# Linear attention on alternating row and column halves, an earlier first product in the convolution, a later first spreading

## The chip, the cores and the metric

The kernel runs on one core of one Trainium2 chip. The metric is the device time of one execution in microseconds; of several runs the median counts. Engines are named as in the profile: PE is TensorE's matmuls, PEld its weight loads, DVE VectorE, ACT ScalarE, POOL GpSimd, SP the engine that issues most loads.

## The reference

Two blocks act on a sequence of 512 frames of width 1024. Cut to the stages that the change touches:

```python
def gla_chunked(q, k, v, g_log):          # 4 heads, key width 64, value width 128, chunks of 64
    q_dec = qc * jnp.exp(bc); k_dec = kc * jnp.exp(-bc)
    A = jnp.einsum('bhnck,bhnsk->bhncs', q_dec, k_dec)
    A = jnp.where(tril, A, 0.0)
    o_intra = jnp.einsum('bhncs,bhnsv->bhncv', A, vc)
    dS = jnp.einsum('bhnck,bhncv->bhnkv', kc * jnp.exp(b_last - bc), vc)
    ...                                    # scan: S = decay * S + dS
    o_inter = jnp.einsum('bhnck,bhnkv->bhncv', q_dec, s_prev)
    o = o_intra + o_inter

def parallel_mixer(xn, ...):
    proj = xn @ w_in                       # xn = rms_norm(h)
    ...                                    # fox attention; gla_chunked; rms_norm of both per head
    return jnp.concatenate([fox_out, gla_o * silu(gr)], axis=-1) @ w_out

def conformer_conv(x, ...):
    a = glu(x @ w_pw1 + b_pw1); y = depthwise_conv(a, width 31) + b_dw
    return silu(layernorm(y, ln_g, ln_b)) @ w_pw2 + b_pw2
```

Around them stand memory cross attention, an MLP, two gated feed-forward blocks and banded attention, which the change leaves alone.

## The kernel before

Activations lie feature-major: eight tiles of 128 features by 512 frames. A dense product is done three times in fp32r, on a high and a low part of both operands (mm3: L396, L397, L398 in the profile), as 128x512 matmuls. Weights come as tiles of 512 KB (raw), one load each on SP's queue; ACT casts the high part (wH, L374) and DVE subtracts the low part (wL, L375), up to four units ahead.

PE runs in the order in which the program is written. In the mixer a helper, drive, mixes a stage (a generator) with a queue of dense products: each yield of the stage gives a number, and dense products are put in until they make up for it. ACT, DVE and POOL get their order from a scheduler, which goes by the program's dependences; in the convolution's second half it is as written.

gla_front does the first norm and the projections of linear attention (GLA). The input norm's factor is a row of 512 numbers; it is spread to all partitions by two matmuls against diagonal tiles: diagonal_pair makes eight 128x128 tiles dg (L1305, DVE), spread multiplies them with ones (L1312) and copies the result to rbc. z, the narrow product times rbc (L945), feeds L960; the narrow product (L465) packs four groups of 32 columns into the array.

gla_back takes GLA's chunks. state(c) adds up one chunk of 64 frames: four matmuls with 64 rows (frames) and 64 columns (keys of a head), to one bank. scores(bp, j) takes two blocks of 128 frames and the two heads on row half j: four matmuls of 64 rows, 128 columns. Behind them, per (bp, j), four times: one full matmul of the masked scores att with gv (L1077), then two quarter matmuls, qd with the states sprev, one for each column half (L1081). ACT copies each output bank to oo (L1084), head_norm squares, sums and scales oo (L742, L743, L751; odd rows on POOL), and L1093 transposes oo to features. The queries and keys of fox attention go through head_norm as well (tm_rows at L732, then L757 transposes them). All of these small products are in plain FP32, in which the trace shows two passes a matmul.

In the convolution, pc sums the taps (L1418, 72 passes of 128x128 in its last group). Layer norm then gives cY (L1551), turn(t) transposes tile t (L1556), gate(t) applies the activation on ACT (cz, L1561) and splits the tile (L540, L541), and the second projection, fm_steps on four banks with their weights W, takes one tile k at a time. keep_warm (L473) runs products on a constant tile, as many as WARM says: at the program's start, ahead of the first transposes, and after those of tile 2.

Of the kernel before, what the change touches and what calls it, by code (L numbers as in the profile page):

```python
# [21 lines left out]
P = 128  # L22
# [45 lines left out]
WARM = (16, 14, 8)  # L68
# [203 lines left out]
class Builder:  # L272
# [653 lines left out]
    def gla_front(self, pool, chl, selr, E):  # L926
# [11 lines left out]
        more(2, G1, 8)  # L938
        rb = self.spread(dg)
# [15 lines left out]
        more(3)  # L955
# [66 lines left out]
    def gla_back(self, pool, gm, E):  # L1022
# [9 lines left out]
        def scores(bp, j):  # L1032
            rs = slice(j * 64, j * 64 + 64)
            att = pool.tile([P, 2, 2, P], F32, tag="att", name=self.nm("att"), bufs=4)
            nc.gpsimd.memset(att, 0.0)
            ps = self.bank().rearrange("p (a t c) -> p a t c", a=2, t=2)
            for a in range(2):
                ts = slice((2 * bp + a) * P, (2 * bp + a + 1) * P)
                for t in range(2):
                    nc.tensor.matmul(ps[:, a, t, :], lhsT=kd[rs, t, ts], rhs=qd[rs, t, ts], start=True, stop=True)  # L1040
            nc.vector.copy_predicated(att, gm.unsqueeze(1).unsqueeze(1).to_broadcast([P, 2, 2, P]), ps)
            atts[bp, j] = att


        def state(c):
            b, rs = c // 2, slice((c % 2) * 64, (c % 2) * 64 + 64)
            ps = self.bank()
            for t in range(2):
                for j in range(2):
                    hs, h = slice(j * 64, j * 64 + 64), 2 * t + j  # L1050
                    nc.tensor.matmul(ps[hs, t * P:(t + 1) * P], lhsT=k2t[rs, b, t, hs], rhs=gv[rs, b, h * P:(h + 1) * P],
                                     start=True, stop=True)
            for t in range(2):
                src = ps[:, t * P:(t + 1) * P]
                if c == 0:
                    nc.vector.tensor_copy(sprev[:, t, 1, :], src)
                else:
                    nc.vector.scalar_tensor_tensor(sprev[:, t, c + 1, :], sprev[:, t, c, :], dec[:, t, c:c + 1], src,
                                                   ALU.mult, ALU.add)

        for c in range(7):
            state(c)
            if c >= 3:
                scores((c - 3) // 2, (c - 3) % 2)
            yield 2.0
        on = []
        for bp in range(2):
            oo = [self.tmp([P, 2, 2, P], name="oo") for _ in range(2)]
            for j in range(2):
                rs = slice(j * 64, j * 64 + 64)  # L1070
# [303 lines left out]
    def ph_con(self, ph):  # L1374
        nc, tc = self.nc, self.tc
        x = self.x
        with tc.tile_pool(name="pc", bufs=1) as pool:
# [118 lines left out]
            with tc.manual_schedule():  # L1496
# [77 lines left out]
                for t in range(1, NT):  # L1574
# [9 lines left out]
                    elif t + 2 < NT:  # L1584
                        turn(t + 2)
# [220 lines left out]
```

## Time and profile before

| | us |
|---|---|
| median of 3 runs | 1883.09 (1882.87 to 1883.69) |
| profiled execution | 1882.25 |
| its span, first to last instruction | 1880.5 |
| PE busy | 1856.4 (99%) |
| DVE, ACT, POOL busy | 976.9, 692.7, 239.7 |

PE is busy nearly throughout, mostly with products in mm3 form. A busy PE is not at its peak: two matmuls that use different parts of the array can overlap, and a matmul at the lower clock is busy for longer.

### The profile page before, as it was taken

How to read it: one execution, taken by the hardware profiler on the slowest of the kernel's cores; microseconds unless marked ns; L12 is line 12 of the kernel's file. 1: busy time of each engine (PE TensorE's matmuls, PEld its weight loads, DVE VectorE, ACT ScalarE, POOL GpSimd, SP SyncE). 2: the span in 40 equal slices, each digit the busy share in tenths (PEclk: the TensorE clock that was granted, in tenths of full speed). 3: DMA queues.
4: the chain of work that ended last, by engine and by line, in shares of the span. 5: the costliest groups of instructions: out<-in, count | busy, mean ns of one | idle time of the engine just before them, and what ended most of it. 6: DMA issues, size and time to landing. Idle time of an engine off the chain costs nothing.

```text
span 1880.5 us, 23226 instructions
## 1 busy us (share of the span) xinstructions
PE 1856.4 (99%) x9174; PEld 1522.9 (81%) x9175; DVE 976.9 (52%) x1690; ACT 692.7 (37%) x1136; POOL 239.7 (13%) x237
## 2 busy tenths in 40 slices
PE   9999999999999999999999999999999999999997
PEld 6878778888888888888788888888877888888886
DVE  6548855765343434486655434335677543343434
ACT  5536653544232324321243222123566432232232
POOL 0102002010000000200021101011254211010110
PEclk9999999999999999999999999999999999999998
DMA  5213322122332322446223332664211223223321
GB/s 195 88 53 117 109 70 99 57 90 90 101 100 92 101 96 95 168 159 220 85 90 104 106 101 88 108 157 140 89 59 46 79 90 101 91 97 92 101 91 55
DMA packets 60653, 191.32 MB, mean 102 GB/s; under 512 B 6352, under 2 KB 16592, under 8 KB 58752
## 3 DMA queue, kind: packets, MB, share of 16 engines
q1 hardware_dynamic: 55152, 169.04, 27.7%
q0 software_dynamic: 2720, 17.83, 3.6%
q10 hardware_dynamic: 2672, 2.97, 0.5%
q8 instruction: 72, 1.18, 0.3%
q14 instruction: 37, 0.30, 0.0%
HBM read 182.90 MB, written 6.91 MB: 101 GB/s over the span
## 4 chain that ended last, share of the span: by engine, by line
PE 88%; DVE 4%; issue 4%; ACT 2%; DMA 1%; POOL 0%; SPq 0%; POOLq 0%; ACTq 0%; DVEq 0%
PE mm L396 26%; PE mm L397 26%; PE mm L398 26%; PE pc L1418 3%; DMA raw<-in_w_dram 1%; DVE wL L375 1%; PE bo L1759 1%; DVE q L1667 1%; PE fs L880 1%; PE ft L895 1%; ACT wH L374 1%; PE fo L908 1%; PE bs L1716 0%; PE ps L506 0%; PE bt L1742 0%
## 5 line engine op out<-in xcount | busy, mean ns | idle before, releaser
L374 ACT CAST wH<-raw 128x1024 fp32r<-128x1024 f32 (+1 forms) x304 | 315.5, 1041 | 890.8 <-PE mm L397 625.9
L396 PE MATMUL mm<-xH,wH 128*128 128x512 f32 x1232 | 481.5, 391 | 0.0
L398 PE MATMUL mm<-xH,wL 128*128 128x512 f32 x1232 | 479.6, 389 | 0.0
L397 PE MATMUL mm<-xL,wH 128*128 128x512 f32 x1232 | 479.6, 389 | 0.0
L375 DVE TENSOR_TENSOR wL<-raw,wH 128x1024 fp32r<-128x1024 f32 (+1 forms) x304 | 372.1, 1225 | 113.5 <-ACT wH L374 106.4
L396 PEld LDWEIGHTS mm<-xH,wH 128*128 128x128 f32 x1232 | 231.3, 188 | 48.9 <-issue 1.7
L398 PEld LDWEIGHTS mm<-xH,wL 128*128 128x128 f32 x1232 | 231.3, 188 | 48.4
L397 PEld LDWEIGHTS mm<-xL,wH 128*128 128x128 f32 x1232 | 231.4, 188 | 47.6 <-DVE xL L537 0.2
L396 PE MATMUL mm<-hidH,wH 128*128 128x512 f32 (+1 forms) x615 | 238.0, 387 | 0.0
L397 PE MATMUL mm<-hidL,wH 128*128 128x512 f32 (+1 forms) x615 | 237.8, 387 | 0.0
L398 PE MATMUL mm<-hidH,wL 128*128 128x512 f32 (+1 forms) x615 | 237.8, 387 | 0.0
L550 DVE TENSOR_TENSOR h<-mm,h 128x512 f32<-128x512 f32 x103 | 71.1, 691 | 262.8 <-PE mm L398 262.8
L499 POOL TENSOR_TENSOR ssq<-ssq,sq 128x512 f32<-128x512 f32 (+1 forms) x49 | 77.7, 1586 | 628.5 <-ACT sq L498 621.8
L1357 POOL TENSOR_TENSOR g<-g,rbc 128x512 f32<-128x512 f32 x44 | 75.1, 1708 | 538.4 <-ACT g L1356 538.4
L396 PEld LDWEIGHTS mm<-hidH,wH 128*128 128x128 f32 x615 | 115.5, 188 | 24.0 <-issue 0.6
L397 PEld LDWEIGHTS mm<-hidL,wH 128*128 128x128 f32 x615 | 115.5, 188 | 23.4
L398 PEld LDWEIGHTS mm<-hidH,wL 128*128 128x128 f32 x615 | 115.5, 188 | 23.4
L1358 DVE TENSOR_TENSOR g<-mm,g 128x512 f32<-128x512 f32 x44 | 30.1, 690 | 124.0 <-PE mm L398 119.4
L1355 DVE TENSOR_TENSOR g<-mm,rbc 128x512 f32<-128x512 f32 x44 | 30.2, 690 | 99.9 <-PE mm L398 98.0
L1324 DVE SCALAR_TENSOR_TENSOR u<-mm,rbc 128x512 f32<-128x512 f32 x32 | 21.9, 691 | 77.0 <-PE mm L398 75.8
L396 PE MATMUL mm<-wH,xH 128*128 128x512 f32 (+1 forms) x160 | 60.8, 380 | 0.0
L398 PE MATMUL mm<-wH,xL 128*128 128x512 f32 (+1 forms) x160 | 59.0, 369 | 0.0
(326 smaller groups left out, 2365.2 us busy)
## 6 DMA issues: line engine op xcount, KB each, us to landing
raw<-in_w_dram SPq DMA_DIRECT2D x272, 512.0 KB, 3.5
mat<-in_mat_dram POOLq DMA_DIRECT2D x14, 1024.0 KB, 6.7
raw<-in_w_dram SPq DMA_DIRECT2D x32, 448.0 KB, 3.2
rel<-rt POOLq DMA_DIRECT2D x1, 3072.0 KB, 36.4
h<-in_x_dram SPq DMA_DIRECT2D x8, 256.0 KB, 5.1
raw<-in_w_dram SPq DMA_DIRECT2D x8, 256.0 KB, 5.2
bias<-rel SPq DMA_DIRECT2D x1, 2048.0 KB, 8.9
mem<-in_mem_dram ACTq DMA_DIRECT2D x4, 256.0 KB, 3.7
```

The source lines that it names most:

```text
L374: self.nc.scalar.copy(H[:, :n], raw[:, :n])
L375: self.low = lambda: self.nc.vector.tensor_tensor(L[:, :n], raw[:, :n], H[:, :n].bitcast(F32), ALU.subtract)
L396: mm(out, lhsT=aH, rhs=bH, start=start, stop=False)
L397: mm(out, lhsT=aH, rhs=bL, start=False, stop=False)
L398: mm(out, lhsT=aL, rhs=bH, start=False, stop=stop)
L499: (eng or nc.gpsimd).tensor_tensor(self.ssq[:, :n], self.ssq[:, :n], q[:, :n], ALU.add)
L550: nc.vector.tensor_tensor(self.h[:, t, :], ps, self.h[:, t, :], ALU.add)
L1324: nc.vector.scalar_tensor_tensor(t, ps, 0.0, rb, ALU.max, ALU.mult)
L1355: nc.vector.tensor_tensor(g, pg, rb, ALU.mult)
L1357: nc.gpsimd.tensor_tensor(g, g, rb, ALU.mult)
L1358: nc.vector.tensor_tensor(g, pu, g, ALU.mult)
L1418: nc.tensor.matmul(ps[:, g * P:(g + 1) * P], lhsT=xs[t][:, g, m:m + P], rhs=matrix(t, g, m), start=m == 0, stop=m == NMAT - 1)
```

## The change

Three places. In gla_front nine matmuls of the projection's fourth bank run ahead of spread, not behind it. In gla_back, states(b) takes both chunks of a block, in two banks, and alternates their row halves and the heads' column halves; scores(bp) alternates the heads' row halves, in two banks; the outputs of a bp take two banks, all eight full matmuls first, then sixteen quarters that alternate row halves and column halves. In the convolution the first bank's product of tile k = t stands ahead of turn(t + 2) from t = 0 on, so that tile 2 is transposed behind the first product and the last two tiles directly one after the other. WARM's three numbers change.

```diff
-WARM = (16, 14, 8)
+WARM = (13, 22, 5)
...
         more(2, G1, 8)
+        more(3, 4, 7)
         rb = self.spread(dg)
...
         ev_k(0)
-        more(3)
+        more(3, 7, 8)
...
-        def scores(bp, j):
-            rs = slice(j * 64, j * 64 + 64)
-            att = pool.tile([P, 2, 2, P], F32, tag="att", name=self.nm("att"), bufs=4)
-            nc.gpsimd.memset(att, 0.0)
-            ps = self.bank().rearrange("p (a t c) -> p a t c", a=2, t=2)
+        def scores(bp):
+
+            banks = []
+            for j in range(2):
+                att = atts[bp, j] = pool.tile([P, 2, 2, P], F32, tag="att", name=self.nm("att"), bufs=4)
+                nc.gpsimd.memset(att, 0.0)
+                banks.append(self.bank().rearrange("p (a t c) -> p a t c", a=2, t=2))
             for a in range(2):
                 ts = slice((2 * bp + a) * P, (2 * bp + a + 1) * P)
                 for t in range(2):
-                    nc.tensor.matmul(ps[:, a, t, :], lhsT=kd[rs, t, ts], rhs=qd[rs, t, ts], start=True, stop=True)
-            nc.vector.copy_predicated(att, gm.unsqueeze(1).unsqueeze(1).to_broadcast([P, 2, 2, P]), ps)
-            atts[bp, j] = att
-
-
-        def state(c):
-            b, rs = c // 2, slice((c % 2) * 64, (c % 2) * 64 + 64)
-            ps = self.bank()
+                    for j in range(2):
+                        rs = slice(j * 64, j * 64 + 64)
+                        nc.tensor.matmul(banks[j][:, a, t, :], lhsT=kd[rs, t, ts], rhs=qd[rs, t, ts], start=True,
+                                         stop=True)
+            for j in range(2):
+                nc.vector.copy_predicated(atts[bp, j], gm.unsqueeze(1).unsqueeze(1).to_broadcast([P, 2, 2, P]),
+                                          banks[j])
+
+
+        def states(b):
+            chunks = [c for c in (2 * b, 2 * b + 1) if c < 7]
+            banks = [self.bank() for _ in chunks]
             for t in range(2):
                 for j in range(2):
                     hs, h = slice(j * 64, j * 64 + 64), 2 * t + j
-                    nc.tensor.matmul(ps[hs, t * P:(t + 1) * P], lhsT=k2t[rs, b, t, hs], rhs=gv[rs, b, h * P:(h + 1) * P],
-                                     start=True, stop=True)
-            for t in range(2):
-                src = ps[:, t * P:(t + 1) * P]
-                if c == 0:
-                    nc.vector.tensor_copy(sprev[:, t, 1, :], src)
-                else:
-                    nc.vector.scalar_tensor_tensor(sprev[:, t, c + 1, :], sprev[:, t, c, :], dec[:, t, c:c + 1], src,
-                                                   ALU.mult, ALU.add)
-
-        for c in range(7):
-            state(c)
-            if c >= 3:
-                scores((c - 3) // 2, (c - 3) % 2)
-            yield 2.0
+                    for i in range(len(chunks)):
+                        rs = slice(i * 64, i * 64 + 64)
+                        nc.tensor.matmul(banks[i][hs, t * P:(t + 1) * P], lhsT=k2t[rs, b, t, hs],
+                                         rhs=gv[rs, b, h * P:(h + 1) * P], start=True, stop=True)
+            for c, ps in zip(chunks, banks):
+                for t in range(2):
+                    src = ps[:, t * P:(t + 1) * P]
+                    if c == 0:
+                        nc.vector.tensor_copy(sprev[:, t, 1, :], src)
+                    else:
+                        nc.vector.scalar_tensor_tensor(sprev[:, t, c + 1, :], sprev[:, t, c, :], dec[:, t, c:c + 1],
+                                                       src, ALU.mult, ALU.add)
+
+        for b in range(4):
+            states(b)
+            if b in (1, 2):
+                scores(b - 1)
+            yield 3.5
         on = []
         for bp in range(2):
             oo = [self.tmp([P, 2, 2, P], name="oo") for _ in range(2)]
+            banks = [self.bank().rearrange("p (a t c) -> p a t c", a=2, t=2) for _ in range(2)]
+
             for j in range(2):
-                rs = slice(j * 64, j * 64 + 64)
-                ps = self.bank().rearrange("p (a t c) -> p a t c", a=2, t=2)
                 for a in range(2):
-                    b = 2 * bp + a
                     for t in range(2):
                         h = 2 * t + j
-                        o = ps[:, a, t, :]
-                        nc.tensor.matmul(o, lhsT=atts[bp, j][:, a, t, :], rhs=gv[:, b, h * P:(h + 1) * P],
-                                         start=True, stop=False)
-                        for i in range(2):
-                            c = 2 * b + i
-                            nc.tensor.matmul(o[i * 64:(i + 1) * 64, :], lhsT=qd[rs, t, c * 64:(c + 1) * 64],
-                                             rhs=sprev[rs, t, c, :], start=False, stop=True)
+                        nc.tensor.matmul(banks[j][:, a, t, :], lhsT=atts[bp, j][:, a, t, :],
+                                         rhs=gv[:, 2 * bp + a, h * P:(h + 1) * P], start=a + t == 0, stop=False)
+
+            for a in range(2):
+                for t in range(2):
+                    for i in range(2):
+                        c = 2 * (2 * bp + a) + i
+                        for j in range(2):
+                            rs = slice(j * 64, j * 64 + 64)
+                            nc.tensor.matmul(banks[j][i * 64:(i + 1) * 64, a, t, :],
+                                             lhsT=qd[rs, t, c * 64:(c + 1) * 64], rhs=sprev[rs, t, c, :],
+                                             start=False, stop=a + t == 2)
+            for j in range(2):
                 for a in range(2):
-                    nc.scalar.copy(oo[a][:, :, j, :], ps[:, a, :, :])
-                yield 2.0
+                    nc.scalar.copy(oo[a][:, :, j, :], banks[j][:, a, :, :])
+            yield 4.0
             on += [o.rearrange("p t j v -> p (t j v)") for o in oo]
...
                 normalise(1, 1)
                 turn(1)
                 gate(0)
-                normalise(2)
-                turn(2)
                 self.keep_warm(ps4[0], WARM[2])
-                for t in range(1, NT):
-                    gate(t)
-                    if t < 5:
-                        drain(self.fm_steps(ps4[0], W[0], yy, [t - 1], 0, 7))
-                        if t + 2 < NT:
-                            if t % 2 == 0:
-                                normalise(t + 2)
-                            turn(t + 2)
-                        for c in range(1, 4):
-                            drain(self.fm_steps(ps4[c], W[c], yy, [t - 1], 0, 7))
-                    elif t + 2 < NT:
+                for t in range(NT):
+                    if t > 0:
+                        gate(t)
+                    if t + 2 < NT:
+                        if t % 2 == 0:
+                            normalise(t + 2)
+                        if t < 4:
+                            drain(self.fm_steps(ps4[0], W[0], yy, [t], 0, 7))
                         turn(t + 2)
+                    for c in range(1, 4) if t < 4 else ():
+                        drain(self.fm_steps(ps4[c], W[c], yy, [t], 0, 7))
```

What the order of the two programs shows at three places. On PE, the first output group of GLA, with the dense products around it (mm); ps is the output's bank. Before:

```order
L397 MATMUL mm_776<-wL_731,xH_155 128x512
L398 MATMUL mm_776<-wH_730,xL_156 128x512
L1077 MATMUL ps_962<-gv,att_859 128x128
L1081 MATMUL ps_962<-sprev,qd 64x128 x2
L1077 MATMUL ps_962<-gv,att_859 128x128
L1081 MATMUL ps_962<-sprev,qd 64x128 x2
```

After:

```order
L397 MATMUL mm_773<-wL_728,xH_152 128x512
L398 MATMUL mm_773<-wH_727,xL_153 128x512
L1085 MATMUL ps_959<-gv,att_844 128x128 x4
L1085 MATMUL ps_960<-gv,att_847 128x128 x4
L1094 MATMUL ps_959<-sprev,qd 64x128
L1094 MATMUL ps_960<-sprev,qd 64x128
```

Before, two such steps repeat this pair of rows, a full matmul and two quarters, in one bank, and a dense row follows. After, eight full matmuls stand together, in two banks, and the quarters behind them go from bank to bank (six more pairs like the last two rows).

On DVE, the head norms of the outputs (oo), with the small operations s of their square root ahead, and the low parts fkL of fox attention's keys. Before:

```order
L487 SCALAR_TENSOR_TENSOR s_1124<-s_1126,s_1124 128x16
L485 TENSOR_TENSOR s_1126<-s_1124 128x16
L486 SCALAR_TENSOR_TENSOR s_1126<-s_1126,s_1110 128x16
L487 SCALAR_TENSOR_TENSOR s_1124<-s_1126,s_1124 128x16
L751 TENSOR_TENSOR oo_960<-oo_960,s_1124 128x512
L751 TENSOR_TENSOR oo_1016<-oo_1016,s_1124 128x512
L375 TENSOR_TENSOR wL_1212<-raw_1078,wH_1211 128x1024
L801 SCALAR_TENSOR_TENSOR fkL_1182<-ps_1183,cst,fkH_1181 128x4x128
L801 SCALAR_TENSOR_TENSOR fkL_1182<-ps_1190,cst,fkH_1181 128x4x128
```

After:

```order
L801 SCALAR_TENSOR_TENSOR fkL_1179<-ps_1180,cst,fkH_1178 128x4x128
L485 TENSOR_TENSOR s_1123<-s_1121 128x16
L801 SCALAR_TENSOR_TENSOR fkL_1179<-ps_1187,cst,fkH_1178 128x4x128
L486 SCALAR_TENSOR_TENSOR s_1123<-s_1123,s_1107 128x16
L801 SCALAR_TENSOR_TENSOR fkL_1179<-ps_1194,cst,fkH_1178 128x4x128
L487 SCALAR_TENSOR_TENSOR s_1121<-s_1123,s_1121 128x16
L801 SCALAR_TENSOR_TENSOR fkL_1179<-ps_1201,cst,fkH_1178 128x4x128
L485 TENSOR_TENSOR s_1123<-s_1121 128x16
L486 SCALAR_TENSOR_TENSOR s_1123<-s_1123,s_1107 128x16
L487 SCALAR_TENSOR_TENSOR s_1121<-s_1123,s_1121 128x16
L751 TENSOR_TENSOR oo_957<-oo_957,s_1121 128x512
L751 TENSOR_TENSOR oo_1013<-oo_1013,s_1121 128x512
```

The rows on oo stood ahead of a split (wL) and the four on fkL; now they stand behind these, and the small operations between them.

On PE, the convolution's transposes (ct, one row for a tile), the warm-up products (warm) and the first products of the second projection. Before, the transposes of tiles 0 to 2:

```order
L1556 MATMUL ct_7427<-kst,cY 128x128 x4
L1556 MATMUL ct_7436<-kst,cY 128x128 x4
L1556 MATMUL ct_7449<-kst,cY 128x128 x4
L473 LDWEIGHTS warm
L473 MATMUL mm_7378<-warm 128x512
```

and behind the eighth of the warm-ups:

```order
L473 LDWEIGHTS warm
L473 MATMUL mm_7378<-warm 128x512
L396 MATMUL mm_7378<-ycH_7419,wH_7029 128x512
L397 MATMUL mm_7378<-ycL_7420,wH_7029 128x512
L398 MATMUL mm_7378<-ycH_7419,wL_7030 128x512
L1556 MATMUL ct_7469<-kst,cY 128x128 x4
L396 MATMUL mm_7379<-ycH_7419,wH_7154 128x512
```

After:

```order
L1571 MATMUL ct_7432<-kst,cY 128x128 x4
L1571 MATMUL ct_7441<-kst,cY 128x128 x4
L473 LDWEIGHTS warm
L473 MATMUL mm_7375<-warm 128x512
...
L396 MATMUL mm_7375<-ycH_7424,wH_7026 128x512
L397 MATMUL mm_7375<-ycL_7425,wH_7026 128x512
L398 MATMUL mm_7375<-ycH_7424,wL_7027 128x512
L1571 MATMUL ct_7462<-kst,cY 128x128 x4
L396 MATMUL mm_7376<-ycH_7424,wH_7151 128x512
```

The third row of transposes stood ahead of the warm-ups; it now stands behind them and behind the first product, ahead of the same products as the fourth row did.

## Rows read from the trace of the kernel before

**Rows 1.** The page's chain that ended last: shares of the span by engine.
```profile
PE 88%; DVE 4%; issue 4%; ACT 2%; DMA 1%; POOL 0%; SPq 0%; POOLq 0%; ACTq 0%; DVEq 0%
```
**Rows 2.** Timeline, start to first spreading: start us, us, engine line op, count [idle before <-releaser].
```profile
0.92 6.40 PE L473 MATMUL ps<-warm 128*128 128x512 bf16 x16 [0.92 <-DVE warm L584]
...
28.86 1.23 DVE L375 TENSOR_TENSOR wL<-raw,wH 128x1024 fp32r<-128x1024 f32 x1 [0.86 <-ACT wH L374]
...
30.68 1.65 DVE L1305 TENSOR_SCALAR dg<-kst,s 128x128 fp32r<-128x128 f32 x8
...
31.60 0.49 PE L1312 MATMUL ps<-dg,ones_r 128*128 128x512 f32 x1 [2.13 <-DVE dg L1305]
...
32.38 0.50 PE L1312 MATMUL ps<-dg,ones_r 128*128 128x512 f32 x1 [0.29 <-DVE dg L1305]
...
37.47 0.68 DVE L945 TENSOR_TENSOR z<-mm,rbc 128x512 f32<-128x512 f32 x1
...
40.91 1.88 PE L960 MATMUL ps<-z,wg 128*128 128x512 f32 x4
```
**Rows 3.** Timeline of PE in GLA, and of the convolution's last taps.
```profile
86.21 0.50 PE L396 MATMUL mm<-wH,xH 128*128 128x512 f32 x1
...
89.06 0.50 PE L396 MATMUL mm<-wH,xH 128*128 128x512 f32 x1
...
94.75 1.16 PE L1040 MATMUL ps<-qd,kd 64*128 64x128 f32 x8
...
112.86 0.50 PE L396 MATMUL mm<-wH,xH 128*128 128x512 f32 x1
...
118.09 0.50 PE L396 MATMUL mm<-wH,xH 128*128 128x512 f32 x1
...
906.61 8.20 PE L1418 MATMUL pc<-mat,xp 128*128 128x128 f32 x72
```
**Rows 4.** Timeline of PE: the narrow product, and one score step of fox attention.
```profile
25.95 1.92 PE L465 MATMUL mm<-h,wn 128*32 128x512 f32 x16
...
204.44 0.40 PE L880 MATMUL fs<-fkL,fqH 64*128 64x512 f32 x2
```
**Rows 5.** Timeline of ACT, PE and POOL around the head norms.
```profile
124.30 0.69 ACT L732 ACTIVATE row<-mm,rcol 128x512 f32<-128x512 f32 x1 [0.24 <-PE mm L398]
...
130.70 0.39 PE L396 MATMUL mm<-wH,xH 128*128 128x512 f32 x1
...
135.95 2.93 POOL L751 TENSOR_TENSOR row<-row,s 128x512 f32<-128x512 f32 x2 [77.08 <-DVE s L486]
...
138.18 1.91 PE L757 MATMUL ps<-kst,row 128*128 128x128 f32 x16
...
145.41 0.60 PE L1093 MATMUL ps<-kst,oo 128*128 128x128 f32 x4
```
**Rows 6.** Timeline in the convolution; in the last, a window's PEclk is the granted clock.
```profile
914.87 3.01 PE L473 MATMUL mm<-warm 128*128 128x512 bf16 x13
...
919.61 1.87 PE L1556 MATMUL ct<-kst,cY 128*128 128x128 f32 x8 [1.73 <-DVE cY L1551]
...
923.28 1.35 PE L1556 MATMUL ct<-kst,cY 128*128 128x128 f32 x4 [1.80 <-DVE cY L1551]
...
924.43 3.62 PE L473 MATMUL mm<-warm 128*128 128x512 bf16 x8
...
928.70 0.60 PE L1556 MATMUL ct<-kst,cY 128*128 128x128 f32 x4
...
941.42 0.78 ACT L1561 ACTIVATE cz<-ct,cst 128x512 f32<-128x512 f32 x1 [1.08 <-PE ct L1556]
...
942.88 0.69 DVE L541 TENSOR_TENSOR ycL<-cz,ycH 128x512 fp32r<-128x512 f32 x1 [1.81 <-ACT ycH L540]
...
943.63 0.19 PEld L397 LDWEIGHTS mm<-ycL,wH 128*128 128x128 f32 x1 [0.38 <-DVE ycL L541]
...
924.00:928.00 4.00, 4.00 (x11) 1.78 (x12) 2.57 (x7) 1.40 (x2) 0.00 (x0) 0.50 0.00 0
```

## The prediction

> **What bounds the kernel now.** I read the chain of work that ended last first: TensorE holds 88% of it [rows 1]. So a microsecond is gained only where TensorE stands still or does passes that can overlap. The timeline of TensorE's stretches that the change touches came next, each against what the other engines finish there; then the order of both programs, for what now stands between a producer and its waiter. From before I need one unit: from 130.70 to 138.18, 33 products of 128x512 lie back to back [rows 5], 7.48/33 = 0.227 us each. A gain on TensorE is kept to the end, because in the stages behind (attention, cross attention, the feed-forward blocks) the other engines are started by TensorE's own results and shift with it; where I found one that doesn't, it is priced below.
>
> **First spreading.** TensorE waits 2.13 for the first four diagonal tiles (dg, L1305), runs one spread matmul, waits 0.29 for the rest, and runs the other [rows 2]. The change puts nine products ahead of these: 9 x 0.227 = 2.04 of work into a wait of 2.42. The order on VectorE moves too: the split L375 waits 0.86 for ScalarE and ends at 28.86 + 1.23 = 30.09; dg begins at 30.68 [rows 2], and the 0.59 between hold four small operations. Three of these now stand ahead of the split, in its wait, so dg comes some 0.4 earlier. Gain 2.04 + 0.4 = **2.4**; bounds 2.0 (dg not earlier) and 2.4 (the whole wait). What is late next is z (L945), ready at 37.47 + 0.68 = 38.15 and read by L960, which would now come at 40.91 - 2.4 = 38.5 [rows 2]: it fits by 0.35.
>
> **Three warm-up products fewer at the start.** The 16 took 6.40, 0.40 each [rows 2], so TensorE begins 1.2 earlier at most. But this stretch ends at dg, and dg stands behind a split that waits for ScalarE's cast of a load [rows 2], not for TensorE. I take 0; bounds 0 and a gain of 0.5, about one spread matmul [rows 2].
>
> **GLA regrouped.** Its FP32 matmuls of 128 columns cost two passes each; 72 such passes of full size took 8.20 [rows 3], 0.114 a pass, and I call that a slot. The old cost of a group is a period less the products in it:
> - state: 89.06 - 86.21 = 2.85, less nine products (2.04), is 0.81 [rows 3]. Four quarter matmuls are eight passes, two column halves at a time four slots, 0.45; the other 0.35 is going into the shape and out of it. Seven of them: 5.7.
> - scores: eight passes one after the other took 1.16 with their tail [rows 3], eight slots and 0.2, so 1.1; four of them: 4.4.
> - output: 118.09 - 112.86 = 5.23, less 2.04, is 3.19 [rows 3]; four: 12.8. Its 8 full passes and 16 quarter passes (two at a time) are 16 slots, 1.8; the other 1.4 is the eight changes between full and quarter shape, 0.17 each.
>
> Together 22.9. Now: row halves alternate in scores, and row and column halves in states and outputs. Four states groups of 16 passes (the last has 8), four at a time, are four slots and 0.35: 4 x 0.81 = 3.2. Two scores groups of 16 passes, two at a time: 2 x 1.1 = 2.2. Two output groups: 16 full passes, then 32 quarter passes four at a time in eight slots, and one way in and out, 24 x 0.114 + 0.35 = 3.1 each: 6.2. Together 11.6, a gain of **11.3**. That halves overlap has two rows: the narrow product on four column groups does 16 matmuls of 512 columns in 1.92, and two score matmuls on two row halves take 0.40, which is the time that one 128x512 matmul has in the product rows [rows 4]. Rows and columns halved together don't occur in this trace. If four quarters go only two at a time, states need 4 slots more in three groups, outputs 8 more in two: 28 x 0.114 = 3.2, and the gain is 8.1. That is the lower bound; the upper one, 12, is the way in and out at half its price.
>
> The Trainium skill ("TensorEngine Tiling (Array Packing)", Tiling Modes) says that a 64x64 grid is four tiles that work independently, and that changing the mode, not the tile, drains the engine. No run here shows the first yet; by it the 11.3 stand, and without it the 8.1.
>
> **What this takes back: the head norms.** The key rows of fox attention run ScalarE, VectorE and GpSimd in series: the last scaling at 124.30, small operations, the multiplications on VectorE and, the later ones, on GpSimd from 135.95 to 138.88; TensorE reaches the transposes (L757) at 138.18 [rows 5]. Its transposes take 0.48 per row, so it needs the last row at 138.18 + 3 x 0.48 = 139.6, and had 0.7 in hand. The chain is not shorter now, but TensorE comes sooner: between key rows and transposes it has 16 product triples (48 x 0.227 = 10.9), where before there was an output block too (3.19). 3.2 - 0.7 = 2.5; the order moves a cast of the chain behind two more copies and a split behind the square sums, both inside slack of up to 0.3 either way: I take 2.2. The gated outputs follow the same path. Before, their multiplications (oo) came ahead of four fkL operations; now they stand behind the four and one split on VectorE, about 3 later, and the oo transposes at 145.41 [rows 5] had 2.2 in hand. 3.0 - 2.2 = 0.8, say 1.0. Loss **3.2**; bounds 0 (slack of other work takes all) and 4.5 (nothing was in hand).
>
> **Convolution.** Before: 14 warm-up products (13 records, 3.01), a wait of 1.73, transposes of tiles 0 and 1, a wait of 1.80, tile 2's, then eight warm-up products of 0.45 each and the first products; those eight ran at a granted clock of 0.50, the lower level of 1.2 GHz, and the next transposes began at 928.70 [rows 6]. After: the eight that are added behind 917.88 end at 917.88 + 8 x 0.227 = 919.7, so the wait before tile 0 (919.61) is filled and tile 0 all but undelayed. Tiles 0 and 1 end at 921.5 as before, five warm-ups end at 922.6, the three matmuls of the first product (0.7) lie in what was the wait for tile 2, and tile 2's transposes, which VectorE feeds from 923.28 on, let the next work begin at 924.43, as they did [rows 6]. That is the work that stood at 928.70: 4.27 ahead. At the end it loses some: the last two transposes, which had nine products between them, are now back to back, so the last split (0.69 from 942.88), which TensorE waited for by 0.38 [rows 6], comes later against it: ScalarE's part of a tile takes 942.88 - 941.42 = 1.46, the transposes of one 0.60 [rows 6], so the last tile's is held up by some 0.8 more. Gain 4.27 - 0.8 = **3.5** with the clock at 2.4 GHz.
>
> **The sum.** 2.4 + 0 + 11.3 - 3.2 + 3.5 = 14.0. The profiled execution took 1882.25, so 1868.25; it stands 0.84 below the median of the runs, 1883.09. The forecast is 1869.1, written 1869.0. Its own range, from the smaller bounds of spread and head norms, is 1866.5 to 1871.
>
> **The rivals.**
> - Quarters go two at a time only: -8.1 in place of -11.3, so 1872.2. For it: no row shows four. Against it: column halves and row halves each overlap [rows 4]. 0.14.
> - The clock falls in the convolution as before. It had fallen after the 1.73 wait, with nothing but transposes and a further wait behind it; from 924 to 928 it was 0.50 [rows 6]. Now the first wait is full of products, but eight transposes still lie ahead of the five warm-ups. If they run at 1.2 GHz until about 928 again, nearly all of the 3.5 goes: a gain of 0.4, so 1872.1. 0.12. The Trainium skill ("TensorE: Matmul & The Clock Gate", Part 4: PE-mode transpose) says that transposes don't count as busy time for the clock in the way that products do. The trace agrees in so far as the clock fell over them, but there the waits lay beside them, so it can't be told which did it.
> - The change doesn't do what it says: row halves don't overlap in this form. Scores lose 2.2 and the quarters 3.2; the GLA gains 5.9, so 1874.5. Against it: L880 does [rows 4]. 0.06.
> - The head norms take nothing (0 for 3.2): 1865.8. 0.05.
> - Slower: each change of the row half drains the array. 16 scores, 28 states and 32 output matmuls, 76, change it. One after the other they need 60 x 0.17 + 16 x 0.114 = 12.0 more than I gave them, and 0.17 of drain each (the price from the output block) 12.9 more; the later TensorE would find the head norms ready (-3.2). 1869 + 24.9 - 3.2 = 1890.7. It decides from 17.2/76 = 0.23 a matmul; between 0.18 and 0.28 the time is within 0.2% of before. Against it: in the state rows column halves change at every matmul without such a price, and L880 changes the row half [rows 3, 4]. 0.07, of which 0.03 within 0.2%.
>
> **How the numbers follow.** The forecast has the other 0.56. 0.2% (3.8 us) is about what a measurement of this kernel can tell from no change; every case but the last lies under 1879.3. Faster 0.93, same 0.03, slower 0.04. A range from 1865.5 to 1873.0 holds the forecast's case and the ones at 1872.2, 1872.1 and 1865.8, less some of their edges: 0.8.
>
> **What would show it.** In the changed trace: the wait of TensorE before L1327 gone (under 0.3 in both); a states group of 16 passes in about 0.45 of run time, an output group of 48 passes in about 2.8; a wait of about 2 before the key transposes and about 1 before those of oo; a granted clock of 1.00 from 920 to 928 in the convolution's stretch (some 10 earlier in time) and a wait near 1 before the last split's product. I am wrong if quarter passes are spaced as full ones, if a wait above 3 stands before the key transposes, or if the clock drops there again.

## The result, and the profile after

| | us |
|---|---|
| before, median | 1883.23 (4 runs, 1882.87 to 1883.69) |
| changed, median | 1868.37 (4 runs, 1868.0 to 1869.69) |
| ratio, with 95% interval | 0.9922 (0.9905 to 0.9939) |
| profiled execution of the changed kernel, its span | 1869.69, 1867.9 |

The forecast was 1869.0, with a range from 1865.5 to 1873.0. A second set of runs, told of below, gave 1870.57 against 1883.16. So the gain is 12.6 to 14.9 us by the two sets; the terms below sum to 13.6. That the first set lies within 0.7 of the forecast is in part luck, since the second lies 1.6 off it. Part of the scatter is the clock in banded attention, which this change doesn't touch: in six of the 13 traces of this study, one of them of the changed kernel, the granted clock reads 0.50 there for a while, and from the end of the convolution's stretch to the end of the program these take 897.0 where the other seven take 895.5.

TensorE's waits in the changed kernel come first, those on which the account rests: who waited for whom, by engine and line, with the total, how many, and the longest.

```profile
PE ps L529 <- DVE dg L524: 2.3, 1, 2.3
...
PE mm L397 <- DVE xL L537: 1.0, 1, 1.0
...
PE ps L757 <- DVE row L751: 0.9, 1, 0.9
...
PE ps L1108 <- POOL oo L751: 0.6, 1, 0.6
...
PE ps L757 <- POOL row L751: 0.4, 2, 0.2
...
PE ps L1327 <- DVE dg L1320: 0.2, 1, 0.2
```

The waits of 1.73 and 1.80 for cY and of 2.13 for dg [rows 2, 6] are gone from it; L757 and L1108 (L1093 before) are new, and so is the one of 1.0 for xL at the start, which is taken up in the account of the terms. The timeline of the changed kernel (start, duration, instruction, count, wait ahead), at the start, in GLA and at the head norms:

```profile
25.96 1.05 PE L506 MATMUL ps<-kst,ssq 128*128 128x1 f32 x8
...
84.14 0.67 PE L1060 MATMUL ps<-gv,k2t 64*64 64x128 f32 x16
...
88.96 1.16 PE L1045 MATMUL ps<-qd,kd 64*128 64x128 f32 x16
...
103.80 1.95 PE L1085 MATMUL ps<-gv,att 128*128 128x128 f32 x16
105.68 1.10 PE L1094 MATMUL ps<-sprev,qd 64*64 64x128 f32 x32
...
113.97 1.20 ACT L1099 COPY oo<-ps 128x256 f32<-128x256 f32 x4 [2.82 <-PE ps L1094]
115.03 0.72 ACT L732 ACTIVATE row<-mm,rcol 128x512 f32<-128x512 f32 x1
...
125.33 0.39 PE L398 MATMUL mm<-wH,xL 128*128 128x512 f32 x1
...
125.89 2.93 POOL L751 TENSOR_TENSOR row<-row,s 128x512 f32<-128x512 f32 x2 [65.96 <-DVE s L485]
...
126.62 0.63 PE L757 MATMUL ps<-kst,row 128*128 128x128 f32 x4 [0.90 <-DVE row L751]
127.43 1.26 PE L757 MATMUL ps<-kst,row 128*128 128x128 f32 x8 [0.18 <-POOL row L751]
128.88 0.66 PE L757 MATMUL ps<-kst,row 128*128 128x128 f32 x4 [0.19 <-POOL row L751]
129.29 0.47 PE L396 MATMUL mm<-wH,xH 128*128 128x512 f32 x1
...
134.63 0.39 PE L398 MATMUL mm<-wH,xL 128*128 128x512 f32 x1
134.86 0.61 PE L1108 MATMUL ps<-kst,oo 128*128 128x128 f32 x2
135.70 0.33 PE L1108 MATMUL ps<-kst,oo 128*128 128x128 f32 x1 [0.22 <-DVE oo L751]
136.59 0.33 PE L1108 MATMUL ps<-kst,oo 128*128 128x128 f32 x1 [0.57 <-POOL oo L751]
136.68 0.48 PE L396 MATMUL mm<-wH,xH 128*128 128x512 f32 x1
```

GLA's first state before, one chunk:

```profile
85.62 0.65 PE L1051 MATMUL ps<-gv,k2t 64*64 64x128 f32 x8
```

To be seen: two chunks' states, 16 passes, take 0.67, about the time that 8 took for one chunk before; 32 quarter passes of an output group take 1.10, less than the 1.95 of its 16 full passes. One score group takes 1.16 for 16 passes, as long as one of 8 did [rows 3]. Before the key transposes a wait of 0.90 now stands, and two of 0.18 and 0.19 lie in them. ScalarE scales the last key row (L732) at 115.03, right behind its copies of the outputs (L1099).

The same in the convolution, with two windows of the changed kernel (the third number from the end is the granted clock):

```profile
905.57 4.97 PE L473 MATMUL mm<-warm 128*128 128x512 bf16 x22
...
910.54 1.87 PE L1571 MATMUL ct<-kst,cY 128*128 128x128 f32 x8
...
912.25 1.25 PE L473 MATMUL mm<-warm 128*128 128x512 bf16 x5
...
914.37 1.06 PE L1571 MATMUL ct<-kst,cY 128*128 128x128 f32 x4
```

```profile
908.00:912.00 4.00, 4.00 (x19) 1.86 (x17) 3.62 (x19) 0.90 (x2) 0.00 (x0) 1.00 0.00 0
912.00:916.00 4.00, 3.93 (x18) 2.24 (x18) 2.61 (x7) 2.83 (x5) 0.00 (x0) 1.00 0.00 0
```

The clock stays at its upper level (2.4 GHz), and neither set of transposes waits. In the kernel before, two windows show where it had fallen:

```profile
920.00:922.00 2.00, 1.48 (x7) 0.76 (x7) 1.09 (x5) 1.31 (x3) 0.00 (x0) 0.84 0.00 0
922.00:924.00 2.00, 0.72 (x3) 0.53 (x3) 1.88 (x5) 1.38 (x3) 0.00 (x0) 0.50 0.00 0
```

A mean of 0.84 is 0.64 us at 0.50, so the clock fell at about 921.4: at the end of the first eight transposes (919.61 to 921.48) [rows 6], and not in the wait for tile 2 behind them.

### The profile page after: what moved, and what is told of

It is laid out like the page before. It is cut to its first block, busy times and chain, and to the rows that moved or that the text cites. A ratio compares the mean times of both kernels' runs of the same rounds, so it can differ in the third digit from the quotient of the medians.

```text
span 1867.9 us, 23231 instructions
## 1 busy us (share of the span) xinstructions
PE 1845.1 (99%) x9177; PEld 1515.9 (81%) x9177; DVE 974.4 (52%) x1690; ACT 692.8 (37%) x1136; POOL 240.5 (13%) x237
## 4 chain that ended last, share of the span: by engine, by line
PE 88%; issue 4%; DVE 4%; ACT 2%; DMA 1%; POOL 1%; SPq 0%; POOLq 0%; ACTq 0%; DVEq 0%
PE mm L396 26%; PE mm L397 26%; PE mm L398 26%; PE pc L1433 3%; DMA raw<-in_w_dram 1%; DVE wL L375 1%; PE bo L1771 1%; DVE q L1679 1%; PE fs L880 1%; PE ft L895 1%; PE fo L908 1%; ACT wH L374 1%; PE ps L506 0%; PE bs L1728 0%; PE bt L1754 0%
```

## The experiments

A whole time hides steps of this size behind what differs from execution to execution at the start and in banded attention, so three stretches of the trace are compared. In kernels whose code is the same there and ahead of it they agree to 0.2 us (front, 58.07 to 58.27) and 0.1 (GLA, 90.52 to 90.63; convolution, 74.88 to 74.95). Each row is one trace:

- front: from the sums of squares (first L506 row) to GLA's first state row;
- GLA: from that row to the first score row of fox attention (L880);
- convolution: from the last row of 72 taps to the next L506 row.

| kernel | front | GLA | convolution |
|---|---|---|---|
| before | 60.65 | 98.13 | 78.42 |
| changed | 58.18 | 90.52 | 74.94 |
| changed_again | 58.27 | 90.63 | 74.94 |
| e_spread_old | 60.13 | | |
| e_warm16 | 58.77 | | |
| e_gla_old | | 98.14 | |
| e_row_halves_apart | | 91.31 | |
| e_shapes_in_turn | | 92.65 | |
| e_fkw20_y15 | | 86.96 | |
| e_conv_old_warm22 | | | 77.85 |
| e_conv_new_warm14 | | | 74.95 |
| e_conv_old_fill | | | 74.79 |
| combined | | 86.96 | 73.80 |

**The spreading undone.**

```diff
-        more(3, 4, 7)
         rb = self.spread(dg)
...
-        more(3, 7, 8)
+        more(3)
```

> The changed kernel with the nine products back behind the first spreading. Theory (they fill the wait for dg): from TensorE's sums of squares (L506) to the first gate product (the line that reads z) 15.7 us as in the kernel before, in place of 13.35, and what follows keeps its length: 2.4 longer. Rival (z or the rows behind it would have been late anyway): less than 1 longer.

The waits are back, the first of them shorter than the 2.13 before [rows 2]; timeline of e_spread_old:

```profile
31.81 0.49 PE L1326 MATMUL ps<-dg,ones_r 128*128 128x512 f32 x1 [1.60 <-DVE dg L1319]
```

The front is 1.95 longer than in the changed kernel, not 2.4: that is the 2.04 of the nine products in the prediction, and the other 0.5 of the 2.47 that the front gained is here too. In this kernel VectorE's split still stands behind all but one of the small operations of dg's chain, so that part of the gain does not come with the nine products. It goes with the warm-ups at the start: in e_warm16, the next run, the nine products stand ahead, but four of the small operations stand behind the split again, as before, and the front is 0.59 longer than in the changed kernel.

**The warm-ups at the start.** WARM is (16, 22, 5).

> The changed kernel with 16 warm-up products at the start. In the five traces with 13, TensorE's first product began at 5.9 to 6.2 (before, with 16: 6.94), but the sums of squares came at 25.07 to 25.96 (before: 24.96). Theory (the loads of the first tiles set that point, and differ from run to run): sums of squares between 24.9 and 26.0 again, the rest as in the changed kernel. Rival (three products fewer cost about as much as they save): sums of squares at 24.96 or earlier.

The sums of squares came at 24.36, earlier than in any other trace, which is the rival's side. But GLA's first state stood at 83.13, and in the kernels with 13 warm-ups and the nine products ahead it stood at 82.97 (e_gla_old) to 84.50 (e_fkw20_y15), 83.61 in the mean. So the early sums brought nothing beyond that spread further on, where dg hangs on a cast; one execution doesn't settle the few tenths between.

**The old GLA.** states, scores and outputs as before, all else as changed.

> The changed kernel with the old GLA (states by chunk, scores and outputs by row half, full and quarter matmuls in turn). Theory (the GLA's own gain is 11.1 and the head norms take 3.5 of it): 7.6 longer than the changed kernel from the key transposes at the front to the first fox scores, no wait before the transposes of the fox keys and of oo. Rival (the head norms' waits come from something else in the change): the waits stay and it is 11 longer.

GLA took 98.14, 7.62 longer, and both waits were gone: the key transposes ran in one piece of 1.91, those of oo began at once. Timeline of e_gla_old:

```profile
135.53 1.91 PE L757 MATMUL ps<-kst,row 128*128 128x128 f32 x16
142.76 0.60 PE L1094 MATMUL ps<-kst,oo 128*128 128x128 f32 x4
```

**Row halves apart.** In states and outputs, all quarters of one row half first:

```diff
+            for i in range(len(chunks)):
+                rs = slice(i * 64, i * 64 + 64)
-            for t in range(2):
-                for j in range(2):
-                    hs, h = slice(j * 64, j * 64 + 64), 2 * t + j
-                    for i in range(len(chunks)):
-                        rs = slice(i * 64, i * 64 + 64)
+                for t in range(2):
+                    for j in range(2):
+                        hs, h = slice(j * 64, j * 64 + 64), 2 * t + j
```

and j as the outermost loop of the output quarters.

> The changed kernel, but in states and outputs all quarter matmuls of one row half come before those of the other, so that neighbours differ in the column half only; scores and everything else stay. Theory (four quarters run at once in the changed kernel): a states group of two chunks takes 8 slots of 0.114 and no longer 4, an output group's 32 quarter passes 16 slots in place of 8, so GLA gets 28 slots or 3.2 us longer, less up to 1.5 that the waits before the head norms' transposes give back. Rival (two at a time in either order, the gain came from the single way in and out): no longer. Rival (neighbours need only differ in anything): no longer than 0.5 us.

None of the three came for the whole of GLA, which is 0.79 longer. Timeline of e_row_halves_apart:

```profile
83.24 0.68 PE L1060 MATMUL ps<-gv,k2t 64*64 64x128 f32 x16
...
104.81 1.59 PE L1094 MATMUL ps<-sprev,qd 64*64 64x128 f32 x32
```

The states take 0.68, as with alternating halves (0.67): four quarters run at once although four of one row half stand ahead of four of the other. The outputs, where eight of one half stand ahead of eight of the other, take 1.59 and not 1.10, 0.49 longer each. Of these 0.98 the whole stretch shows 0.79. So quarters do run four at a time, as the forecast had it, but it is not the alternation that brings it in the states: by the spacing of their single records the second half starts 0.03 behind the first, which is not nearly through. So TensorE doesn't start these matmuls in the order in which the program has them. In the outputs it starts 0.50 behind, when ten of the first half's 16 passes have begun, and only the last six run beside it.

**Full and quarter shapes in turn.** Each output group runs two full matmuls and their four quarters, four times over.

```diff
-            for j in range(2):
-                for a in range(2):
-                    for t in range(2):
+            for a in range(2):
+                for t in range(2):
+                    for j in range(2):
...
-            for a in range(2):
-                for t in range(2):
-                    for i in range(2):
+                    for i in range(2):
```

> The changed kernel, but an output group runs two full matmuls, then their four quarters, four times over, in place of eight full ones and then sixteen quarters. The passes are the same. Theory (a change between full and quarter shape costs about 0.17 us, as worked out from the old output group): six more changes a group, so 1.0 us a group and 2.0 in all, less what the later waits give back. Rival (the old group's excess was the quarters' own, not the change of shape): 0.

GLA is 2.13 longer, which over twelve more changes of shape is 0.18 each. (The order of the two banks and the accumulation flags change along with the shapes; the 0.17 from the old output group, which took one bank at a time, is the check on that.) Timeline of e_shapes_in_turn, half of one such group:

```profile
102.96 0.60 PE L1085 MATMUL ps<-gv,att 128*128 128x128 f32 x4
103.50 0.45 PE L1091 MATMUL ps<-sprev,qd 64*64 64x128 f32 x8
103.88 0.71 PE L1085 MATMUL ps<-gv,att 128*128 128x128 f32 x4
104.52 0.45 PE L1091 MATMUL ps<-sprev,qd 64*64 64x128 f32 x8
```

The waits gave nothing back: 0.89 stood before the key transposes again. So the head norms' chain moves with the end of GLA and is no slack for time lost in it.

**More products ahead of the key transposes.** FKW = 20 for 16, and 15.0 for the yield of 12.0 behind head_norm.

> The changed kernel with four product triples more (12 matmuls, 2.7 us of TensorE) ahead of the transposes of fox attention's key rows, and as many triples as before between these and the transposes of oo, which the order on VectorE then scales ahead of the four low parts of the keys. The products are taken from those that follow. Theory (the head norms' chain runs from the end of the GLA outputs, and TensorE comes 2.1 and 1.5 too early to its ends): both waits go, 3.0 to 3.5 us in all. Rival (the chain is held by TensorE's own products, so that it moves with them): no gain, the waits stay or move to the transposes of the query rows.

GLA took 86.96, 3.56 less than in the changed kernel, a little more than expected, and both waits were gone. Timeline of e_fkw20_y15:

```profile
128.63 1.91 PE L757 MATMUL ps<-kst,row 128*128 128x128 f32 x16
135.86 0.60 PE L1108 MATMUL ps<-kst,oo 128*128 128x128 f32 x4
```

**The convolution: order and warm-ups apart.** Three kernels: the old order with 22 warm-ups at first and eight behind tile 2; the new order with 14 and five; and the old order with 22, and the eight moved ahead of tile 2 (the third against the first):

```diff
                 gate(0)
+                self.keep_warm(ps4[0], WARM[2])
                 normalise(2)
                 turn(2)
-                self.keep_warm(ps4[0], WARM[2])
```

> The changed kernel with the convolution's old order (tile 2's transposes and eight warm-ups ahead of the first product) and 22 warm-ups ahead of tile 0. The wait of 1.7 before tile 0 is filled, the one of 1.8 before tile 2 stays. If the transposes with one such wait are enough for the clock to fall, the granted clock reads 0.50 some 2 us behind tile 0's transposes again and the stage is 3.5 to 4 us longer than in the changed kernel; if it needed the first wait, the clock stays at 1.00, the eight warm-ups take 1.8 in place of 3.6, and the stage is 1.5 to 2 us longer.

> The changed kernel with 14 warm-ups ahead of tile 0, as before, so that TensorE waits some 1.7 there again; the new order of products stays. If the wait ahead of the transposes brings the clock down, the granted clock reads 0.50 in some of the stretch behind them and the stage is 2 to 3 us longer than in the changed kernel; if the second wait did, the clock stays at 1.00 and the stage keeps its length within 0.3 us, since VectorE sets when tile 0 can be turned.

> The changed kernel with the convolution's old order of products (22 warm-ups ahead of tile 0), but its eight later warm-ups between the transposes of tile 1 and tile 2, where TensorE waited 1.8, and not behind tile 2's. Theory (the clock falls over transposes and a wait without a product between, and what the changed order gains is the fill of this wait): granted clock 1.00 throughout, the stage from the last taps to the next sums of squares 66.9 to 67.4 us (69.8 with the eight behind tile 2, 66.9 in the changed kernel). Rival (the first product's place ahead of tile 2 is what counts): 68 or more at a clock of 1.00.

The first had no wait ahead of tile 0, and the clock fell all the same, later than in the kernel before: behind the wait for tile 2 (912 to 914 reads 0.94, so at about 913.8). The stretch is 2.91 longer than in the changed kernel, not 3.5 to 4. Its timeline and a window:

```profile
909.73 1.87 PE L1571 MATMUL ct<-kst,cY 128*128 128x128 f32 x8
913.40 1.35 PE L1571 MATMUL ct<-kst,cY 128*128 128x128 f32 x4 [1.80 <-DVE cY L1566]
914.55 3.20 PE L473 MATMUL mm<-warm 128*128 128x512 bf16 x8
```

```profile
914.00:916.00 2.00, 2.00 (x7) 0.95 (x7) 0.82 (x2) 1.18 (x2) 0.00 (x0) 0.50 0.00 0
```

The second had the wait of 1.74 ahead of tile 0, and the clock stayed; the stretch is as long as in the changed kernel (74.95 and 74.94). Its timeline and window:

```profile
909.45 1.87 PE L1571 MATMUL ct<-kst,cY 128*128 128x128 f32 x8 [1.74 <-DVE cY L1566]
911.15 1.25 PE L473 MATMUL mm<-warm 128*128 128x512 bf16 x5
```

```profile
912.00:914.00 2.00, 1.94 (x9) 0.91 (x8) 2.00 (x6) 1.22 (x2) 0.00 (x0) 1.00 0.00 0
```

The third, in the old order of products, took 74.79, a little less than the changed kernel. Its timeline and window:

```profile
911.83 1.91 PE L473 MATMUL mm<-warm 128*128 128x512 bf16 x8
```

```profile
912.00:914.00 2.00, 1.94 (x9) 0.73 (x7) 1.37 (x4) 1.90 (x3) 0.00 (x0) 1.00 0.00 0
```

Its eight warm-ups ran in 1.91, where those behind tile 2 had taken 3.20 and 3.62 [rows 6]. (The stretches in the expectations are counted from the end of the taps and so about 8 shorter.) So the order of the products is not what gained the 3.5, and the 22 warm-ups gave 0.57 of it in the old order (78.42 to 77.85) and nothing in the new one. The rest, 3.06, is there as soon as TensorE has products to run between tile 1 and tile 2, warm-ups or others: 1.29 of it is the eight warm-ups' own time at the two clocks (3.20 and 1.91), and the other 1.77 is about the wait of 1.80 that they now fill.

What brings the clock down these runs don't settle. Before tile 2 the kernel before and e_conv_new_warm14 have the same 14 warm-ups, a wait of 1.73 or 1.74 and eight transposes; the clock fell at the end of these in the one and not in the other, where products followed at once. Each is one execution, and banded attention, whose code all kernels share, fell to 0.50 in six traces and not in seven. It did not fall in the convolution in any of the 11 traces that have products between tile 1 and tile 2, and it did in the two that have none.

**The two last, timed in five rounds.** The changed kernel once more, and one that adds the FKW edit and this, in the second projection:

```diff
+            for t in range(4):
+                drain(self.fm_steps(ps4[t], W[t], yy, range(4, 6), 0, 7))
             for t in range(NT):
                 if t < 4:
-                    drain(self.fm_steps(ps4[t], W[t], yy, range(4, 8), 0, 7))
+                    drain(self.fm_steps(ps4[t], W[t], yy, range(6, 8), 0, 7))
```

> The changed kernel once more, timed beside the kernel before in five rounds on one chip, as the measure for the next one. Both theories: 13 to 15 us under before (13.6 by the terms read from the trace: spreading 2.4, GLA 11.1, head norms -3.5, convolution 3.5).

> The changed kernel with the four product triples moved ahead of the key transposes (3.6 us shorter between GLA and fox attention in the one look at it), and in the convolution's second projection the last four tiles taken in two steps over the first four banks, tiles 4 and 5 for all, then 6 and 7, so that the last two splits have 24 products of cover and not 6. Theory: the waits of 0.2 to 0.5 for tiles 6 and 7 go, about 1.0 less in the convolution, 4.6 under the changed kernel and 18 under before. Rival (the weights of the first four banks, held longer, delay the next unit): the convolution no shorter, 3.6 under the changed kernel.

| kernel | median | runs | ratio to before, 95% interval |
|---|---|---|---|
| before | 1883.16 | 9 | |
| changed | 1870.57 | 5 | 0.9928 (0.9915 to 0.9942) |
| combined | 1865.25 | 4 | 0.9904 (0.989 to 0.9917) |

The changed kernel gained 12.6, a little under what was expected; the traces of this set, of both kernels, had the lower clock in banded attention for a while. The combined one gained 17.9, and 5.3 over the changed one: 3.56 in GLA and 1.14 in the convolution by the stretches (4.7), the rest within the scatter. It is the fastest kernel of this study.

## Why the prediction was right, step by step

| term | forecast | by the trace |
|---|---|---|
| spreading | 2.4 gained | 2.47 (front, 60.65 to 58.18) |
| warm-ups at the start | 0 | not told apart from 0, not in the sum |
| GLA | 11.3 gained | 11.14 |
| head norms | 3.2 lost | 3.53 |
| convolution | 3.5 gained | 3.48 (78.42 to 74.94) |
| sum | 14.0 | 13.6 |

GLA: from its first state row to the last product ahead of the key transposes lie 132 products in both kernels; it took 137.95 - 85.62 = 52.33 before and 125.33 - 84.14 = 41.19 after. The row of before that closes this stretch and the one behind the key transposes [rows 5] are these, from its timeline:

```profile
137.95 0.39 PE L398 MATMUL mm<-wH,xL 128*128 128x512 f32 x1
...
139.85 0.48 PE L396 MATMUL mm<-wH,xH 128*128 128x512 f32 x1
```

The groups came out one by one as well. Four rows of the changed kernel, each the first product behind a group:

```profile
84.74 0.50 PE L396 MATMUL mm<-wH,xH 128*128 128x512 f32 x1
...
90.05 0.50 PE L396 MATMUL mm<-wH,xH 128*128 128x512 f32 x1
...
100.27 0.50 PE L396 MATMUL mm<-wH,xH 128*128 128x512 f32 x1
...
106.71 0.50 PE L396 MATMUL mm<-wH,xH 128*128 128x512 f32 x1
```

Between the first two lie 15 products (3.41), a states group and a score group: 5.31 - 3.41 = 1.90, where the forecast has 0.81 + 1.1. Between the last two lie 15 products and an output group: 6.44 - 3.41 = 3.03, forecast 3.1.

Head norms: from the last product ahead of the key transposes to the first behind them, 1.90 before and 129.29 - 125.33 = 3.96 after, so 2.06 lost (forecast 2.2). The working had the chain no shorter; from the last key row's scaling to GpSimd's last row it is 13.79 (115.03 to 128.82), against 14.58 before (124.30 to 138.88) [rows 5]. Around the first transposes of oo, 0.58 before (the products at 145.18 and 145.76) and 136.68 - 134.63 = 2.05 after, so 1.47 lost (forecast 1.0). The term was mis-sized there by half: the forecast took only how late the last rows come. The waits shown there are 0.22 and 0.57; the rest is that the first two of four transposes ran, stood, and began again. The wait table alone (2.1 for both places) would understate the loss of 3.5.

The profiled execution gained 1882.25 - 1869.69 = 12.56, less than the sum, because its front came late: its sums of squares stood at 25.96 (24.97 before), with TensorE waiting 1.0 for xL. 12.56 + 1.0 is the 13.6 of the terms. In the eleven traces with 13 warm-ups these sums lie between 24.73 and 26.34, 25.47 in the mean, and all eleven have a wait for xL ahead of them, of 0.53 to 1.03; the two with 16 (before and e_warm16) have none, and their sums stand at 24.97 and 24.36. So a part of this may be no spread but the price of the three warm-ups, and the term of 0 the sum of a loss here and of the 0.5 that dg gained and that the table books under spreading. Two traces with 16 don't show it.

Convolution: the two parts came out. The second bank's first product began 22.45 behind the last taps before and begins 17.65 behind them now, 4.8 earlier; one tile's transposes less, 0.36, stand ahead of it, so 4.4 are gained (forecast 4.27). Of these 1.0 is lost again towards the end (forecast 0.8). But that happens at the splits of tiles 6 and 7, where the waits are 0.19 and 0.23; the wait near 1 before the last split, which was to show it, didn't come. Two more signs came in another size. A states group shows 0.67, not 0.45, since its row goes to the end of the last pass (the starts lie within 0.40), and the wait before the key transposes is 0.90, the rest of the 2.06 lying in the stops behind it.

Three things did not hold as reasons, though the numbers came out:

- In the convolution, the working put the gain down to the order of the products and to the first wait's fill. The old order with its warm-ups in the gap gains as much (74.79), and with the first wait back the stretch is as long (74.95). Of the rival on the clock, eight transposes with products right behind them left it at 1.00; what brought it down before stays open. The Trainium skill ("TensorE: Matmul & The Clock Gate", Part 4: PE-mode transpose) says that transposes don't count as busy time in the way that products do; the trace agrees in this much, that the clock fell over transposes before and in e_conv_old_warm22, and these runs don't tell them from the waits beside them.
- In GLA, four at a time was right, but the alternation of halves, to which the working ties it, was not needed in the states (0.68 against 0.67); in the outputs it was (1.59 against 1.10).
- In the expectations of two experiments I took the head norms' waits for slack that a longer GLA would use up. It used 0.2 of 0.98 in one and nothing of 2.13 in the other, because the chain's last scaling stands right behind ScalarE's copies of the last outputs (115.03), and moves with their end. What does help is work put behind the start of the chain: 12 products moved there took both waits away.

Of the rivals, the slower one (a drain at each change of the row half) is excluded by the states, which change it at every matmul and are 0.02 longer for 16 passes than for 8. The price of a change between full and quarter shape, 0.17 in the working, came out at 2.13/12 = 0.18.

## What to carry to other kernels

When a stage on the engine that bounds gets shorter, look for chains on other engines that start at its end and whose end the bound engine meets a fixed amount of work later: the stage's gain shortens that cover, and moving independent products behind the chain's start gives it back (3.56 us here). Small matmuls are worth grouping by shape first and by half second, and a gap in which TensorE waits between transposes is worth filling with anything: here that gave 3.06 us by one pair of runs, of which 1.29 lay in products behind the gap that had run at the lower clock.

## What the runs showed of the hardware

- Four 64x64 quarters run at once (32 passes in 1.10, where 16 of the full array take 1.95), and over a few matmuls the engine does not need them in alternating order: with four matmuls of one row half ahead of four of the other a group of 16 passes takes 0.68, with strict alternation 0.67. With eight ahead of eight, 32 passes take 1.59 in place of 1.10.
- A change between the full array and quarters costs 0.18 us, by twelve of them in one kernel, and 0.17 by the old output groups.
- Transposes that run, wait for a row and begin again cost more than the waits listed: 1.47 for the listed 0.79 at oo, 2.06 for 1.27 at the keys.
- The granted clock fell to 0.50 at the end of eight transposes behind a wait of 1.73 (before), and in the transposes of tile 2, behind eight others and a wait of 1.80 (e_conv_old_warm22). It stayed at 1.00 where five or eight products lay right behind the first eight transposes, in one execution with a wait of 1.74 ahead of these. Which of transposes and waits did it is not shown.
